# A two-layer hybrid mixer: its first stage put into a written order, with rounded first folds and condition vectors in PSUM

## The chip, the core and the metric

The kernel runs on one core of a Trainium2 chip. The core has a matrix engine (TensorE, called PE in the profile; its weight loads are listed apart as PEld), three elementwise engines (VectorE = DVE, ScalarE = ACT, GpSimd = POOL) and SyncE (SP), which issues nearly all DMA transfers. Each engine works through its own list in order and waits on semaphores where it needs another's result. The metric is the device time of one execution in microseconds; lower is better.

## What is computed

Batch 1, 1024 latent tokens (S), 256 context tokens (C), width 1024 (D), two layers. All data is float32. The parts of the reference that matter here:

```python
sc, scc = jax.nn.silu(c), jax.nn.silu(c_ctx)
shift, scale, gate = jnp.split(sc @ mod_w[0] + mod_b[0], 3, axis=-1)
hx = modulate(rmsnorm(x, norm_g[0]), shift[:, None], scale[:, None])
shift_c, scale_c, gate_c = jnp.split(scc @ mod_w[0] + mod_b[0], 3, axis=-1)
hc = modulate(rmsnorm(ctx, norm_g[0]), shift_c, scale_c)

def even_mixer(h, h0, p):                       # layer 0
    va, vg, ga, xb, gb = jnp.split(h @ p["w_in"], [...], axis=-1)
    y_a = conformer_conv(va, vg, p) * jax.nn.silu(ga)   # u = va*sigmoid(vg), 31-tap conv, layernorm, silu
    y_b, hT = rglru_branch(xb, p, h0, True)             # 4-tap conv, two gates in two directions, scan
    y_b = y_b * jax.nn.silu(gb)
    return jnp.concatenate([y_a, y_b], axis=-1) @ p["w_out"], hT
```

The context goes only through the `xb` columns and gives the scan its start. In layer 1 a pooling mixer follows; the product of its input weights with its group weights does not depend on the tokens, and the kernel works it out ahead ("folds"): `wfold[g]` is `wu[g]` times `grp[g]`, for four groups g.

## The kernel before

**Tiles.** Channels lie on the 128 partitions, tokens along the free axis; D is 8 tiles (KT) of 128 channels. A weight tile is 128 x 1024 (512 KB). For precision most products are done three times on rounded operands: a value is split into a high part, rounded to the matmul type fp32r by a copy on ACT, and a low part, the difference, worked out on POOL or DVE; then high x high, high x low and low x high are summed in PSUM (`mm3_steps`, line 128, and `mm3_fixed`, line 522). PSUM has eight banks: four rotate under the name `mm` (`psum`, line 87), two form the wide tile `xb` (`wide`, line 91), two more are `c0` and `c1` (`banks`, line 95).

**First stage, lines 297 to 501.** The two condition vectors are spread over the partitions by a one-row product and end in SBUF as `cL` (latents) and `cC` (context). For 6 of the 8 channel tiles (KD = 6), `modulation(k)` (line 344) loads rows k and 8 + k of the transposed modulation weights and makes four dot products on DVE, two rows by two vectors. For the last two tiles `mod_row` (line 365) makes the same numbers on TensorE from `modW`. `x_load` (line 408) loads a tile of x and adds its squares; `rstd_cols` (line 196) makes the reciprocal root of the mean square of all tokens, spread over the partitions. `modulate(k)` (line 384) then scales a tile of x (DVE), rounds it to `h0h` (ACT) and makes the low part `h0l` (DVE). The context takes the same way (`ctx_load`, `ctx_scale`, `ctx_split`). Meanwhile TensorE folds groups 0 and 1 with `fold_whole` (line 271): 64 matmuls of 512 columns on unrounded float32, each of which the profile records as two. Here a planner orders the instructions of each engine, and only the loads are chained (`load`, line 108).

**Second stage, lines 740 to 890.** From the first `vg` product on, nearly everything passes through `on` (line 506), which ties each instruction behind the one before it on its engine: the order of the text is the order of the engine. Loop j from 0 to 7 makes `vg`, `va` (48 matmuls each), the context part `xbc` of tile j + 1 (24 of 256 columns), and then the twelve gate steps of tile j (`gate_steps`, line 725: three matmuls and one Sigmoid on ACT each), between which stand the 48 matmuls of `xb` for tile j + 1. DVE has the four-tap convolution (`other_taps`, line 674), `u = va * sg`, the scans (`rec_scan`), and in between steps of the 31-tap convolution (`conv`, line 574; 49 steps for a tile j below 5, 50 above), which `fill(n)` (line 651) puts in, n at a time. At j = 0 the eight rows of the gate part of the modulation are loaded and dotted too (line 779), and the loop ends with `fill(19)` (line 836).

**After it** come the products `gb`, the output product `wob` (with `fill(7)` behind each half, line 1209), and at m = 5 the layer norm's mean (`ln_mean`, line 1216), which needs all convolutions done. From there to the end nothing is touched by the change.

Of the kernel before, what the change touches and what calls it, by code (L numbers as in the profile page):

```python
# [9 lines left out]
F32 = mybir.dt.float32  # L10
# [5 lines left out]
P = 128  # L16
S = 1024
# [29 lines left out]
KD = 6  # L47
KR = KT - KD
KW = 4 // ((KR + 1) // 2)


# [4 lines left out]
def body(ctx, tc, xT, ctxT, cc, ccol, modT, modW, win, gw, wout, wu, grp, wg, wo1, small, edge, ident, outT):  # L56
# [37 lines left out]

    def banks(name, n):
        if n % 2:
            t = wide(name)
            return [t[:, h] for h in HALF]
        return [pc.tile([P, H], F32, tag=f"c{i}", name=f"{name}_{i}") for i in range(2)]
# [69 lines left out]
    def decay_rates():  # L169
        nc.scalar.activation(sa, lam, AF.Abs)  # L170
        nc.scalar.activation(sa, sa, AF.Exp, scale=-1.0)
        nc.vector.tensor_scalar(out=sb, in0=sa, scalar1=2.0, scalar2=None, op0=add)
        nc.vector.reciprocal(sb, sb)
        nc.vector.tensor_tensor(out=sz, in0=sa, in1=sb, op=mult)
        nc.vector.tensor_tensor(out=sb, in0=sz, in1=sz, op=mult)
        nc.vector.memset(sa, 1.0 / 17.0)
        for n in range(7, -1, -1):
            nc.vector.tensor_tensor(out=sa, in0=sa, in1=sb, op=mult)
            nc.vector.tensor_scalar(out=sa, in0=sa, scalar1=1.0 / (2 * n + 1), scalar2=None, op0=add)
        nc.vector.tensor_tensor(out=sa, in0=sa, in1=sz, op=mult)  # L180
        nc.vector.tensor_scalar(out=sb, in0=lam, scalar1=-1.0, scalar2=0.0, op0=mult, op1=ALU.max)
        nc.vector.scalar_tensor_tensor(out=sa, in0=sa, scalar=2.0, in1=sb, op0=mult, op1=add)
        nc.vector.tensor_scalar(out=chalf, in0=sa, scalar1=4.0, scalar2=None, op0=mult)
        nc.vector.tensor_scalar(out=cneg, in0=sa, scalar1=-8.0, scalar2=None, op0=mult)
# [86 lines left out]
    def fold_whole(g, out_tile, g_tile, w_tile):  # L271
        gs = []
        for i in range(2):
            raw = g_tile(f"graw_{g}_{i}")
            load(raw, grp[g, i])
            gs += [raw[:, 0:H], raw[:, H:D]]
        yield
        for kp in range(KT // 2):
            w = w_tile(f"wu_{g}_{kp}")
            load(w, wu[g, kp])  # L280
            for s in range(2):
                ps = psum(f"fold_{g}_{kp}_{s}")
                for i in range(4):
                    kc = slice(i * 2 * P + s * P, i * 2 * P + (s + 1) * P)
                    nc.tensor.matmul(ps, w[:, kc], gs[i], start=(i == 0), stop=(i == 3))  # L285
                dst = wfold[g][:, :, 2 * kp : 2 * kp + 2, :]
                o = out_tile(f"fo_{g}_{kp}_{s}")
                nc.scalar.copy(o, ps)
                nc.sync.dma_start(dst[:, :, s, :].rearrange("m p c -> p m c"),
                                  o.rearrange("p (m c) -> p m c", c=P))  # L290
            yield


    EVAC = 1000


    cpool = tc.alloc_tile_pool(name="cpool", bufs=1)
    cth = [cpool.tile([P, D], F32R, name=f"cth{i}") for i in range(2)]
    ctl = [cpool.tile([P, D], F32R, name=f"ctl{i}") for i in range(2)]
    cL = cpool.tile([P, D], F32, name="cL")  # L300
    hh, hl, ch, cl = [], [], [], []
    with ExitStack() as sctx:
        fpool = sctx.enter_context(tc.tile_pool(name="fpool", bufs=6))
        gpool = sctx.enter_context(tc.tile_pool(name="gpool", bufs=4))
        spool = sctx.enter_context(tc.tile_pool(name="spool", bufs=1))

        def fo_tile(name):
            return fpool.tile([P, H], F32, tag="fo", name=name)

        def g_tile(name):  # L310
            return gpool.tile([P, D], F32, tag="g", name=name)

        raws = [0]

        def raw_tile(name):
            tag = ("wr", "wh", "wl")[raws[0] % 3]
            raws[0] += 1
            return wpool.tile([P, D], F32, tag=tag, name=name)

        folds = (u for g in range(2) for u in fold_whole(g, fo_tile, g_tile, raw_tile))  # L320

        def fold_some(n):
            for _ in range(n):
                next(folds, None)

        cC = spool.tile([P, D], F32, name="cC")
        cx = [spool.tile([P, D], F32, name=f"cx_{i}") for i in range(2)]


        xs = []  # L330
        acc = [atile("ssq0"), atile("ssq1")]
        accc = spool.tile([P, C], F32, name="ssqc")

        def sumsq(acc_, v, n, first, name, eng):
            if first:
                nc.scalar.activation(acc_[:, :n], v, AF.Square)
            else:
                q = ttile(name)
                nc.scalar.activation(q[:, :n], v, AF.Square)
                eng.tensor_tensor(out=acc_[:, :n], in0=acc_[:, :n], in1=q[:, :n], op=add)  # L340

        junk = spool.tile([P, D], F32, name="junk")

        def modulation(k, between=lambda: None):
            raws_ = []
            for m in (k, KT + k):
                raws_.append(dtile(f"mod0_{m}"))
                load(raws_[-1], modT[0, m])
                if m == k:
                    between()  # L350
            for m, raw in zip((k, KT + k), raws_):
                for i, vec in enumerate((cL, cC)):
                    nc.vector.scalar_tensor_tensor(out=junk, in0=raw, scalar=1.0, in1=vec, op0=mult, op1=mult,
                                                   accum_out=m0[:, i, m : m + 1])
            nc.vector.scalar_tensor_tensor(out=a0[:, :, k], in0=m0[:, :, KT + k], scalar=mb1[:, k : k + 1],
                                           in1=col(O_NG + k).to_broadcast([P, 2]), op0=add, op1=mult)
            v = m0[:, :, k]
            nc.vector.tensor_tensor(out=v, in0=v, in1=col(O_MB + k).to_broadcast([P, 2]), op=add)

        idx = spool.tile([P, P], F32, name="idx")
        ccv = spool.tile([P, KT, 2], F32, name="ccv")

        def mod_row(j):
            ps = psum(f"modr_{j}")[:2, : KR * P]
            for q in range(KT // KW):
                raw = dtile(f"modw_{j}_{q}")
                load(raw[:, : KW * KR * P], modW[j, q])
                for e in range(KW):  # L370
                    k = KW * q + e
                    nc.tensor.matmul(ps, ccv[:, k], raw[:, e * KR * P : (e + 1) * KR * P],
                                     start=(k == 0), stop=(k == KT - 1))
            row = ttile(f"modrow_{j}")[:2, : KR * P]
            nc.scalar.copy(row, ps)
            pst = psum(f"modt_{j}")[:, : 2 * KR].rearrange("p (m c) -> p c m", c=2)
            for e in range(KR):
                nc.tensor.matmul(pst[:, :, e], row[:, e * P : (e + 1) * P], idx[:2, :2], start=True, stop=True)
            ms = slice(j * KT + KD, (j + 1) * KT)
            nc.vector.scalar_tensor_tensor(out=m0[:, :, ms], in0=pst, scalar=1.0 / D,  # L380
                                           in1=col(O_MB + ms.start, KR).unsqueeze(1).to_broadcast([P, 2, KR]),
                                           op0=mult, op1=add)

        def modulate(k):
            t = xs[k]
            shift = m0[:, 0, k : k + 1]
            for h in range(2):
                nc.vector.scalar_tensor_tensor(out=t[:, HALF[h]], in0=t[:, HALF[h]], scalar=a0[:, 0, k : k + 1],
                                               in1=rx[h], op0=mult, op1=mult)
            th, tl = dtile(f"h0h_{k}", F32R), dtile(f"h0l_{k}", F32R)  # L390
            nc.scalar.activation(th, t, AF.Identity, bias=shift)
            nc.vector.scalar_tensor_tensor(out=tl, in0=t, scalar=shift, in1=th.bitcast(F32), op0=add, op1=sub)
            hh.append(th)
            hl.append(tl)

        last_cast = [None]

        def modulate_ctx(k):
            i, q4 = k // 4, k % 4
            cs = slice(q4 * C, (q4 + 1) * C)  # L400
            nc.gpsimd.tensor_scalar(out=cx[i][:, cs], in0=cx[i][:, cs], scalar1=a0[:, 1, k : k + 1],
# [1571 lines left out]
```

## Time and profile before

| | us |
|---|---|
| median of 3 runs | 1290.15 (1288.58 to 1293.81) |
| span of the profiled execution | 1287.8 |
| TensorE busy | 1271.1 |
| VectorE busy | 1141.3 |
| ScalarE busy | 640.6 |
| GpSimd busy | 354.3 |

The span runs from the first to the last instruction of one execution; the run's time holds a little more around it. A row of the views that group instructions reads: line, engine, operation, output from inputs, shape, count, then busy time, the mean of one in ns, and the engine's idle time just before them with what ended it. Many rows have line 510, since `on` records everything there; the tile names tell them apart (`wh_va` is the high part of weight tile `va`, `wl_va` its low part, `wr_va` the raw load). Matmuls overlap in their pipeline: one of 512 columns is shown with 390 ns, while 48 in a row take 10.88 us.

### The profile page before, as it was taken

What the parts mean: (1) busy time and instruction counts of PE and PEld (TensorE: products, weight loads), DVE (VectorE), ACT (ScalarE), POOL (GpSimd) and SP (SyncE); (2) the same over time, 40 slices, a digit from 0 to 9 for tenths busy, and PEclk for the clock granted to TensorE, in tenths of its full rate; (3) what the DMA queues carried; (4) which work ended last, traced back from release to release, by engine and by line L of the source; (5) the groups of instructions that cost most, each with busy time, mean ns of one, the idle gap of its engine ahead of it and who ended that gap; (6) DMA issues with size and microseconds to landing.
All of it is one profiled execution on the core that took longest, in us unless ns stands there. A gap on an engine that the chain in (4) does not pass through costs nothing.

```text
span 1287.8 us, 15841 instructions
## 1 busy us (share of the span) xinstructions
PE 1271.1 (99%) x5650; PEld 1027.5 (80%) x5650; DVE 1141.3 (89%) x1775; ACT 640.6 (50%) x941; POOL 354.3 (28%) x180
## 2 busy tenths in 40 slices
PE   8999999999999999999999999999999999999997
PEld 4468888888888888888887888888888888878886
DVE  7979999999999999988789667999999997887876
ACT  5343656666657623227426345834444444654543
POOL 3063655675558603443220023000000000000002
PEclk9999999999999999999999999999999999999999
DMA  9934111121212133543555356243333324777723
GB/s 371 358 114 157 58 41 63 44 74 42 66 41 90 50 115 107 168 147 113 172 174 192 127 185 203 87 155 127 110 132 131 123 96 157 245 247 258 296 83 131
DMA packets 83075, 181.87 MB, mean 141 GB/s; under 512 B 7858, under 2 KB 27826, under 8 KB 82996
## 3 DMA queue, kind: packets, MB, share of 16 engines
q1 hardware_dynamic: 74548, 176.67, 40.1%
q10 hardware_dynamic: 8448, 4.20, 1.1%
q8 instruction: 44, 0.72, 0.2%
q14 instruction: 35, 0.29, 0.1%
HBM read 136.79 MB, written 44.04 MB: 140 GB/s over the span
## 4 chain that ended last, share of the span: by engine, by line
PE 86%; DVE 6%; DMA 5%; ACT 1%; issue 1%; SPq 0%; POOL 0%; POOLq 0%; DVEq 0%; ACTq 0%
PE vg L510 7%; PE wob L510 7%; PE gb L510 7%; PE va L510 7%; PE xb L510 6%; PE g L510 4%; PE fold L285 3%; PE ga L510 2%; PE qb_v L1000 2%; PE qb_v L1001 2%; PE qb_v L998 2%; PE xbc L510 2%; PE qb_g L1000 2%; PE qb_g L1001 2%; PE qb_g L998 2%; DMA x<-xT 1%
## 5 line engine op out<-in xcount | busy, mean ns | idle before, releaser
L510 DVE SCALAR_TENSOR_TENSOR conv<-u,sm,conv 128x505 f32<-128x505 f32 (+6 forms) x224 | 153.9, 748 | 0.9
L1762 POOL TENSOR_TENSOR o<-x,rr 128x256 f32<-128x256 f32 (+1 forms) x10 | 9.4, 971 | 445.7 <-ACT rr L1698 443.8
L510 POOL TENSOR_TENSOR l<-l,l 128x1280 f32<-128x1280 f32 (+1 forms) x23 | 64.0, 2798 | 91.8 <-DVE l L510 65.5
L510 ACT ACTIVATE l<-g,sm 128x512 f32<-128x512 f32 (+1 forms) x96 | 58.7, 619 | 57.7 <-PE g L510 57.0
L285 PE MATMUL fold<-graw,wu 128*128 128x512 f32 x128 | 58.0, 614 | 2.3 <-DMA wu<-wu 2.3
L102 ACT CAST wq_g<-wr_g 128x512 fp32r<-128x512 f32 x48 | 28.3, 622 | 48.4 <-DVE wr_g L979 17.6
L285 PEld LDWEIGHTS fold<-graw,wu 128*128 128x128 f32 x128 | 25.1, 198 | 33.7 <-issue 32.7
L510 PE MATMUL vg<-h0h,wl_vg 128*128 128x512 f32 x128 | 50.0, 390 | 0.0
L510 PE MATMUL wob<-ybh,wh_wob 128*128 128x512 f32 x128 | 49.9, 390 | 0.0
L510 PE MATMUL vg<-h0h,wh_vg 128*128 128x512 f32 x128 | 49.8, 389 | 0.0
L510 PE MATMUL gb<-h0l,wh_gb 128*128 128x512 f32 x128 | 49.8, 389 | 0.0
L510 PE MATMUL gb<-h0h,wh_gb 128*128 128x512 f32 x128 | 49.8, 389 | 0.0
L510 PE MATMUL wob<-ybh,wl_wob 128*128 128x512 f32 x128 | 49.8, 389 | 0.0
L510 PE MATMUL vg<-h0l,wh_vg 128*128 128x512 f32 x128 | 49.8, 389 | 0.0
L510 PE MATMUL wob<-ybl,wh_wob 128*128 128x512 f32 x128 | 49.8, 389 | 0.0
L510 PE MATMUL va<-h0h,wh_va 128*128 128x512 f32 x128 | 49.8, 389 | 0.0
L510 PE MATMUL va<-h0l,wh_va 128*128 128x512 f32 x128 | 49.8, 389 | 0.0
L510 PE MATMUL va<-h0h,wl_va 128*128 128x512 f32 x128 | 49.8, 389 | 0.0
L510 PE MATMUL gb<-h0h,wl_gb 128*128 128x512 f32 x128 | 49.8, 389 | 0.0
L510 DVE TENSOR_TENSOR_SCAN l<-l,l 128x256 f32<-128x256 f32 (+1 forms) x32 | 48.7, 1521 | 1.1
L103 POOL TENSOR_TENSOR wl_wu<-wr_wu,wh_wu 128x1024 fp32r<-128x1024 f32 x8 | 19.2, 2417 | 106.9 <-ACT wh_wu L102 104.4
L510 POOL TENSOR_TENSOR l<-l,uc 128x1280 f32<-128x1280 f32 x16 | 48.1, 3032 | 0.0
(642 smaller groups left out, 4344.0 us busy)
## 6 DMA issues: line engine op xcount, KB each, us to landing
mod<-modT SPq DMA_DIRECT2D x20, 512.0 KB, 5.5
x_part<-xp SPq DMA_DIRECT2D x32, 256.0 KB, 3.1
mod<-modT SPq DMA_DIRECT2D x32, 256.0 KB, 3.1
wr_v<-wfold SPq DMA_DIRECT2D x16, 512.0 KB, 4.0
wr_g<-wg SPq DMA_DIRECT2D x16, 512.0 KB, 4.2
wr_wo<-wo SPq DMA_DIRECT2D x16, 512.0 KB, 4.6
y_b<-y SPq DMA_DIRECT2D x24, 256.0 KB, 3.4
y_t<-y SPq DMA_DIRECT2D x24, 256.0 KB, 2.9
```

What stands on the lines that cost most here:

```text
L102: return (nc.scalar.copy(hi, src), eng.tensor_tensor(out=lo, in0=src, in1=hi.bitcast(F32), op=sub))
L103: eng.tensor_tensor(out=lo, in0=src, in1=hi.bitcast(F32), op=sub))
L285: nc.tensor.matmul(ps, w[:, kc], gs[i], start=(i == 0), stop=(i == 3))
L510: last[eng] = f(*args, **kw)
L998: nc.tensor.matmul(ps, hi, xh[k], start=(first and k == 0), stop=False, skip_group_check=not first)
L1000: nc.tensor.matmul(ps, hi, xl[k], start=False, stop=False, skip_group_check=not first)
L1001: mm = nc.tensor.matmul(ps, lo, xh[k], start=False, stop=(k == KH - 1), skip_group_check=not first)
L1762: nc.gpsimd.tensor_tensor(out=outs[k // per][:, k % per], in0=x1[k][:, cols], in1=rr, op=mult)
```

## The change

The first stage is written anew, and every instruction of it now passes through `on`, so that TensorE, DVE, ACT and POOL each follow the order of the text from the first instruction on, and SP that of `load`.

- The folds of groups 0 and 1 are done with split operands, 24 matmuls of fp32r for each of the 8 weight tiles, in place of 8 of float32. The four raw group tiles are split by ACT and DVE, the eight weight tiles by ACT and POOL. The stores stand in the chain of loads.
- The condition vectors stay in PSUM: `cvec[0]` in the wide tile `xb`, `cvec[1]` in a second wide tile `cw`. `cL` is a copy of the first, used for the gate rows and later.
- `mod_row` and its inputs are gone; all 8 tiles have dot products on DVE, for tiles 5 to 7 the latents' first and the context's later.
- The products `xb0` and `vg0` of the latents run together, channel tile by channel tile.
- Behind them stand `va0`, the context's normalisation, `u0`, the decay rates, the gate rows, the gate steps of tile 0 for the latents with `xb1` between them, then `xbc0`, `xbc1` and the gate steps for the context. Iteration j = 0 of the loop is gone, and where it ended with `fill(19)` (and had `fill(3)` before) stands `fill(4)`.

```diff
+    def wide2(name):
+        return pc.tile([P, S], F32, tag="cw", name=name)
...
+    cvec = [wide("c_0"), wide2("c_1")]
...
+    def fold_part(n, s, part):
+        g = n // 4
+        w = fw[n][part == 2]
+        for i in range(4):
+            kc = slice(i * 2 * P + s * P, i * 2 * P + (s + 1) * P)
+            hi, lo = gpair[g][i // 2]
+            x = lo if part == 1 else hi
+            pe(fps_[n][s], w[:, kc], x[:, HALF[i % 2]], start=(part == 0 and i == 0), stop=(part == 2 and i == 3))
...
+    def mod_dots(m, vecs=(0, 1)):
+        for i in vecs:
+            vec(nc.vector.scalar_tensor_tensor, out=mraw[m] if i else junk, in0=mraw[m], scalar=1.0, in1=cvec[i],
+                op0=mult, op1=mult, accum_out=m0[:, i, m : m + 1])
...
+    load_w("vg0", win[KT])
+    load_mod(5)
...
+    mod_dots(5, (0,))
+    for h in range(2):
+        r, t = roots[h], ttile(f"dg_x{h}")
+        vec(nc.vector.reciprocal, out=r, in_=r)
+        vec(nc.vector.tensor_tensor, out=t.rearrange("p (c t) -> p c t", t=P),
+            in0=idx.unsqueeze(1).to_broadcast([P, H // P, P]), in1=r.unsqueeze(2).to_broadcast([P, H // P, P]), op=mult)
...
+    rest = [lambda: (mod_dots(KT + 5, (0,)), mod_ready(0, 4, 6)), lambda: mod_dots(6, (0,)), lambda: mod_dots(KT + 6, (0,)),
+            lambda: (mod_ready(0, 6, 7), mod_dots(7, (0,))), lambda: (mod_dots(KT + 7, (0,)), mod_ready(0, 7, KT)),
+            lambda: (mod_dots(5, (1,)), mod_dots(KT + 5, (1,))), lambda: None, lambda: None]
+    scale_x(0)
+    high_x(0)
+    for k in range(KT):
+        if k < KT - 1:
+            scale_x(k + 1)
+            high_x(k + 1)
+        low_x(k)
+        rest[k]()
+        if k == 0:
+            xb = wide("xb0")
+            vg = [psum(f"vg0_{h}") for h in range(2)]
+        kc = slice(k * P, (k + 1) * P)
+        for part in range(3):
+            for (hi, lo), ps in ((w, [xb[:, h] for h in HALF]), (wg0, vg)):
+                for h in range(2):
+                    pe(ps[h], (lo if part == 1 else hi)[:, kc], (hl if part == 2 else hh)[k][:, HALF[h]],
+                       start=(k == 0 and part == 0), stop=(k == KT - 1 and part == 2))
...
+    first_tap(0, xb, uc[:, C:])
+    sg = [ttile(f"sg0_{h}") for h in range(2)]
+    for h in range(2):
+        act(sg[h], vg[h], AF.Sigmoid)
+    other_taps(0, xb, uc[:, C:])
+    wva = split_w("va0", (cth[0], ctl[0]))
+    uh, ul = utile("uh0", F32R), utile("ul0", F32R)
+    cast(uh[:, C:], uc[:, C:])
+    wnext = split_w("xb1")
+    gp(out=ul[:, C:], in0=uc[:, C:], in1=uh[:, C:].bitcast(F32), op=sub)
+    va = [psum(f"va0_{h}") for h in range(2)]
+    all_of(mm3_fixed(va[0], wva, (hh, hl), HALF[0]))
+    msc = psum("ms_c")[:, :C]
+    pe(msc, ones, accc, start=True, stop=True)
+    all_of(mm3_fixed(va[1], wva, (hh, hl), HALF[1]))
...
+    load(rawg, gw[0])
...
+    load(raw, win[KT + 1])
+    lrows = {m: lrow(m) for m in range(2 * KT, 3 * KT)}
...
+    act(sq, msc, AF.Sqrt, bias=eps_r)
+    lrow_dots(2 * KT)
+    u = xtile("u0")
...
+    vec(nc.vector.tensor_tensor, out=u[:, HALF[0]], in0=va[0], in1=sg[0], op=mult)
+    vec(nc.vector.reciprocal, out=accc, in_=sq)
+    for i in range(2):
+        v = cx[i].rearrange("p (k n) -> p k n", n=C)
+        vec(nc.vector.tensor_tensor, out=v, in0=v, in1=accc.unsqueeze(1).to_broadcast([P, 4, C]), op=mult)
+        for q4 in range(4):
+            k, cs = 4 * i + q4, slice(q4 * C, (q4 + 1) * C)
+            on("pool", nc.gpsimd.tensor_scalar, out=cx[i][:, cs], in0=cx[i][:, cs], scalar1=a0[:, 1, k : k + 1],
+               scalar2=m0[:, 1, k : k + 1], op0=mult, op1=add)
...
+        cast(cth[i], cx[i])
+        gp(out=ctl[i], in0=cx[i], in1=cth[i].bitcast(F32), op=sub)
+    vec(nc.vector.tensor_tensor, out=u[:, HALF[1]], in0=va[1], in1=sg[1], op=mult)
...
+    decay_rates()
...
+    for m in range(2 * KT + 1, 2 * KT + 4):
+        lrow_dots(m)
...
+    for n, _ in enumerate(gate_steps(0, (gwh, gwl), (uh, ul), gates, ((C, H), (C + H, H)))):
+        while done < 16 * (n + 1) // 8:
+            next(steps)
+            done += 1
...
+    all_of(mm3_fixed(xc, w, (ch, cl), slice(0, C)))
...
+    all_of(mm3_fixed(xcn, wnext, (ch, cl), slice(0, C)))
+    first_tap(0, xc, uc[:, :C])
+    other_taps(0, xc, uc[:, :C])
+    cast(uh[:, :C], uc[:, :C])
+    gp(out=ul[:, :C], in0=uc[:, :C], in1=uh[:, :C].bitcast(F32), op=sub)
...
+    first_tap(1, xcn, ucn[:, :C])
+    other_taps(1, xcn, ucn[:, :C])
+    for m in range(2 * KT + 4, 3 * KT):
+        lrow_dots(m)
...
+    all_of(gate_steps(0, (gwh, gwl), (uh, ul), gates, ((0, C),)))
...
+    rec_input(state, 0)
+    w = raw_split(raw, "vg1")
+    at_rest()
+    fill(4)
```

912 lines of the change are left out of this document (488 added, 424 removed).

## The prediction

> **What bounds the kernel now.** I read the page first, then the busy time by stretches, the chain of work that ended last, and DVE's instructions in order of time.
>
> ```profile
> span 1287.8 us, 15841 instructions
> PE 1271.1 (99%) x5650; PEld 1027.5 (80%) x5650; DVE 1141.3 (89%) x1775; ACT 640.6 (50%) x941; POOL 354.3 (28%) x180
> ...
> PE 86%; DVE 6%; DMA 5%; ACT 1%; issue 1%; SPq 0%; POOL 0%; POOLq 0%; DVEq 0%; ACTq 0%
> ```
>
> TensorE looks like the only bound. The stretches (from:to, length, then busy PE, PEld, DVE, ACT, POOL with counts, clock, DMA share, GB/s) correct that:
>
> ```profile
> 0.00:55.00 55.00, 49.50 (x143) 23.86 (x144) 44.84 (x78) 25.10 (x43) 10.52 (x11) 1.00 0.99 376
> ...
> 80.70:102.40 21.70, 21.70 (x107) 18.21 (x106) 13.89 (x33) 9.75 (x12) 14.72 (x12) 1.00 0.46 172
> 102.40:137.50 35.10, 35.10 (x173) 29.74 (x172) 34.85 (x50) 12.12 (x18) 11.74 (x5) 1.00 0.22 75
> 137.50:180.00 42.50, 42.50 (x206) 35.86 (x205) 42.01 (x56) 26.50 (x30) 25.02 (x10) 1.00 0.16 54
> ...
> 521.00:566.00 45.00, 45.00 (x201) 37.24 (x200) 44.37 (x72) 11.59 (x15) 24.32 (x15) 1.00 0.47 158
> ```
>
> Until 55 us the DMA share is 0.99: loads pace the stage. From 102 us on DVE is as full as TensorE (42.01 of 42.5), also in the output product (44.37 of 45). A delay of DVE is therefore not hidden by a faster TensorE. The chain (start, us, what) dates TensorE's side:
>
> ```profile
> 46.27 27.66 PE fold L285 x64
> ...
> 74.37 6.87 PE fold L285 x16
> ...
> 105.96 10.88 PE va L510 x48
> 116.84 2.87 PE xbc L510 x24
> ...
> 137.56 10.88 PE vg L510 x48
> ...
> 166.66 0.35 PE g L510 x3
> ...
> 508.55 65.28 PE wob L510 x288
> ```
>
> Folds fill TensorE until 81 us, then products run without a gap, 0.227 us for a matmul of 512 columns, and tile 1 begins at 137.56. DVE's side (start, us):
>
> ```profile
> 124.58 14.76 DVE L510 SCALAR_TENSOR_TENSOR conv<-u,sm,conv 128x504 f32<-128x504 f32 x22
> 139.24 1.28 DVE L510 SCALAR_TENSOR_TENSOR uc<-xb,sm,uc 128x1022 f32<-128x1022 f32 x1
> ...
> 165.04 1.50 DVE L510 SCALAR_TENSOR_TENSOR uc<-xbc,sm,uc 128x254 f32<-128x254 f32 x3
> ...
> 568.60 0.41 DVE L510 CAST mu0h<-lnsum 128x512 fp32r<-128x512 f32 x1
> ...
> 574.10 0.69 DVE L510 TENSOR_TENSOR mu1l<-lnsum,mu1h 128x512 fp32r<-128x512 f32 x1 [2.68 <-PE mu L510]
> ```
>
> Two couplings are to be seen. DVE frees the bank of `xbc` at 166.5 and the fourth gate step takes it at 166.66: DVE has 0.2 us in hand at tile 1. And DVE begins the layer norm's mean at 568.6, while TensorE ends its first 288 `wob` matmuls at 573.8: with 1.2 us for both parts of the mean's operand DVE has 4.0 us in hand there.
>
> **The change: until the first products.** The rows of the first stage (grouped; mean in ns last before the bar):
>
> ```profile
> L285 PE MATMUL fold<-graw,wu 128*128 128x512 f32 x11 | 7.4, 840 | 2.3 <-DMA wu<-wu 2.3
> ...
> L353 DVE SCALAR_TENSOR_TENSOR junk<-mod,cL 128x1024 f32<-128x1024 f32 x12 | 15.2, 1266 | 1.7 <-DMA mod<-modT 0.8 <-ACT cL L433 0.8
> L388 DVE SCALAR_TENSOR_TENSOR x<-x,a,ms_x 128x512 f32<-128x512 f32 x16 | 10.8, 744 | 0.5 <-PE ms_x L211 0.5
> L392 DVE SCALAR_TENSOR_TENSOR h0l<-x,m,h0h 128x1024 fp32r<-128x1024 f32 x8 | 10.5, 1335 | 0.0
> ...
> L372 PE MATMUL modr<-modw,ccv 128*2 128x256 f32 x32 | 7.2, 379 | 0.0
> ```
>
> TensorE's own work falls: the folds from 64 float32 matmuls at 2 x 0.433 us (27.66 / 64 a record), 55.4 us, to 192 at 0.227, 43.5 us; and 7.2 us of `modr` go. Neither is on the path, for products wait for other things. The order of loads puts 33 half-megabyte loads, 7 stores of 0.26 MB and 0.3 MB of small ones, 19.4 MB, before and with modulation row 5; at 376 GB/s that is 51.6 us. DVE has the dot product of that row in front of the two diagonals: 1.3, then 1.5 for reciprocals and diagonals and 1.0 for spreading them (estimates from the half-width DVE op at 0.68, which is 10.8 / 16, and two float32 matmuls): x is scaled from 55.4 on.
>
> The products are written tile by tile, but `xb0` is the next tile in the banks of `cvec[0]`, and four of that vector's dot products (rows 6, 14, 7, 15) stand in `rest[1]` to `rest[4]`, behind it. TensorE's first matmul, and in its order all others, must wait for the last. Until then DVE runs 12 half scalings (8.1), 5 low parts at 1.31 (6.6), 5 dots at 1.27 (6.3) and two sets of small adds (0.8): 21.8, so products begin at 77. No row has a dot with a PSUM operand: the half-width scaling with one (0.68) doubles to 1.35, the SBUF dot is 1.27 and I take that; a single bank read without gain or loss. Ends: 1.15 and 1.35 a dot, 1 us here either way. The 96 matmuls take 21.8. By then TensorE has stood since its folds ended near 58 (the eighth fold's last 8 matmuls stand behind the spreading). The first 11 fold records after a thin start took 7.4 us, 0.67 each against 0.433, so that start cost 2.6; I take 2.0 here, 1.0 before `va0` and 1.5 at the gates (0 to 2.6 each). Call the end of `xb0` and `vg0` T: 77 + 21.8 + 2.0 = 101. Before, these 96 matmuls would end at 80.7 + 21.8 = 102.5. The gain up to here is 1.5 us.
>
> The Trainium skill (TensorE: Matmul & The Clock Gate, Part 1: The HAM clock gate) says that the array runs at half clock for some 3.4 us after an idle window of that length. The clock column reads 1.00 in the very stretch with the slow records, so the slow start agrees and the column does not show it; an estimate by that page is 1.7 us for each of four restarts, 6.8 in place of my 4.5.
>
> **From T to tile 1.** These rows price it, the engines' groups first and then the loads, with us from issue to landing last:
>
> ```profile
> L510 ACT ACTIVATE uc<-xb,sm 128x1024 f32<-128x1024 f32 x2 | 2.4, 1206 | 0.7 <-PE xb L510 0.7
> L510 ACT ACT_TABLE_LOAD x1 | 1.3, 1283 | 0.0
> L510 ACT ACTIVATE sg<-vg 128x512 f32<-128x512 f32 x2 | 1.2, 600 | 0.8 <-PE vg L510 0.8
> L510 ACT CAST wh_va<-wr_va 128x1024 fp32r<-128x1024 f32 x1 | 1.0, 1044 | 0.0
> L510 POOL TENSOR_TENSOR wl_va<-wr_va,wh_va 128x1024 fp32r<-128x1024 f32 x1 | 2.4, 2395 | 5.8 <-ACT wh_va L510 5.8
> L510 DVE SCALAR_TENSOR_TENSOR uc<-xb,sm,uc 128x1023 f32<-128x1023 f32 x2 | 2.6, 1283 | 0.1
> L193 DVE RECIPROCAL ssqc<-sq_c 128x256 f32<-128x256 f32 x1 | 1.7, 1746 | 0.0
> L443 DVE TENSOR_TENSOR cx<-cx,ssqc 128x1024 f32<-128x1024 f32 x2 | 2.4, 1222 | 0.0
> L401 POOL TENSOR_SCALAR cx<-cx,a,m 128x256 f32<-128x256 f32 x8 | 5.2, 670 | 7.6 <-DVE cx L443 7.6
> L172 DVE TENSOR_SCALAR sb<-sa 128x16 f32<-128x16 f32 x1 | 4.4, 4351 | 7.0 <-ACT sa L171 7.0
> L510 POOL TENSOR_TENSOR l<-l,uc 128x1280 f32<-128x1280 f32 x1 | 3.0, 2974 | 0.0
> L510 DVE SCALAR_TENSOR_TENSOR l<-l,cL 128x1024 f32<-128x1024 f32 x8 | 15.3, 1970 | 0.0
> ```
>
> ```profile
> l<-modT SPq DMA_DIRECT2D x6, 512.0 KB, 6.5
> ...
> wr_vg<-win SPq DMA_DIRECT2D x1, 512.0 KB, 3.4
> wr_va<-win SPq DMA_DIRECT2D x1, 512.0 KB, 4.3
> ```
>
> Wait one, before `va0`: on ACT its cast stands behind the first tap, a table load and two Sigmoids (1.2 + 1.3 + 1.1 + 1.0, with handovers T + 4.8), and POOL's low part ends at T + 7.3. `va0` and the context's sum end at T + 19.5.
>
> Wait two, at the gates: DVE's taps (3 x 1.28) end at T + 5.3, ACT rounds `uh` and `xb1` by T + 7.4, POOL's low part of `xb1` at T + 9.9 frees the raw buffer that SP needs for `vg1`; the gate row 16 is queued behind that load and lands 4.3 later, at T + 14.8 (3.4 for a lone load in the same list, 6.5 in a bunch: -1 to +2). Behind its dot on DVE stand `u0`, the reciprocal and the context's scaling: first half at T + 19.6. POOL's four scalings (2.6), ACT's cast (1.1), POOL's low part (2.4), four more scalings and the second cast give T + 29.6; then come Abs, Exp and two table loads, and only then the first gate's Sigmoid, at T + 33.3. TensorE fills its four banks with gate steps and half of `xb1` by T + 27.7 (36 matmuls, 8.2) and waits 5.6. The other half ends at T + 43.1, `xbc0` and `xbc1` at T + 48.9.
>
> Wait three, before `vg1`: tap, taps, cast and low part of the context (0.6 + 1.5 + 0.4 + 0.7) pass beside `xbc1`; POOL's `rec_input` (3.0, from T + 51) stands ahead of the low part of `vg1` (2.4): T + 56.5. TensorE is at tile 1 as if from 157.3, 19.7 later than 137.56.
>
> DVE: Exp arrives at T + 31.3, the first small op sits out POOL's low part as the 4.35 us row did (T + 32), 22 small ones at 0.2 (T + 37), three gate rows (T + 40.7), the wait for `xbc0` and its taps (T + 48.3), the next taps (T + 51.2), four gate rows beside `rec_input` (1.3 each, 1.97 at worst: T + 56.5), one sum (T + 57.4), and seven convolution steps at 0.67 (14.76 / 22): the taps of tile 1 start at T + 62.1 = 163.1 where they started at 139.24. That is 23.9 later, less the 0.2 in hand: 23.7. It is the larger, so TensorE loses 4 us more in tile 1.
>
> **Behind it.** `fill(4)` for 3 + 19 steps moves 18 steps, 12.0 us, to the `wob` stage. In tiles 1 to 7 nothing changes; at the mean DVE had 4.0 us in hand, so TensorE stands 8.0 longer there.
>
> **Sum:** 23.7 + 8.0 = 31.7 on the span of 1287.8, 1319.5. The median stands 2.35 above that span, so **1322 us**.
>
> **The rivals.** (a) The bank holds nothing up: T = 55.4 + DVE's whole list of 31 us (16 half scalings, 8 low parts, 7 dots) + 1.5 = 88, all else as above: 1309. For: the text order; against: four dots on the old tile. Chance 0.12. (b) Faster: TensorE is the bound throughout, T = 88 and the three waits vanish because ACT and POOL run ahead; then 102.5 - 88 = 14 us are won, 1276. For: 86% of the chain; against: each wait is a queue written out. 0.08. (c) No change: T = 88, DVE's lag is taken up by spare time I do not see, and only TensorE's own waits count, 88 + 56.3 - 137.56 = 7, less 4 if the gate row is there in time: 1293. 0.08. (d) Worse: all restarts cost 2.6, gate rows 1.97 each, rows land late: 1335 and up. 0.10. That leaves 0.62 for my forecast, decided at the point where the taps of tile 1 start: before 131 us the change would win (8 us being lost again at the mean), after that it loses.
>
> Range: 1303 (all of (a)) to 1337; (b), (c) and half of (d) lie outside. Within 0.5%, 6.5 us, is about what a measurement of this kernel cannot tell from no change: faster 0.08, same 0.08, slower 0.84.
>
> **What would show it.** Right: a gap in TensorE between the last fold near 58 us and the first `xb0` matmul near 77, released by DVE's dot; idle TensorE before `va0` (7 us), inside the gate steps of tile 0, and at `vg1`; taps of tile 1 near 163; idle TensorE before `mu`. Wrong: `xb0` starting near 57, gate Sigmoids ahead of the context's casts, or DVE idle in tiles 1 to 7.

## The result and the profile after

| | before | after |
|---|---|---|
| median of the runs beside each other, us | 1289.37 (4 runs, 1287.05 to 1293.81) | 1370.33 (4 runs, 1368.69 to 1374.21) |
| ratio after / before, 95% interval | | 1.0627 [1.0595, 1.066] |
| span of the profiled execution, us | 1287.8 | 1366.9 |

The change costs 81 us; 32 were predicted, and the time lies far above the range (1303 to 1337). First the page of the changed kernel: its span, the busy time, the chain by engine, and the group of convolution taps (busy us, mean ns of one, then idle us before them).

```profile
span 1366.9 us, 15894 instructions
PE 1278.4 (94%) x5674; PEld 1047.1 (77%) x5674; DVE 1175.1 (86%) x1789; ACT 651.4 (48%) x947; POOL 370.2 (27%) x187
...
PE 58%; DVE 23%; issue 7%; ACT 4%; POOL 4%; DMA 4%; POOLq 0%; SPq 0%; DVEq 0%; ACTq 0%
...
L276 DVE SCALAR_TENSOR_TENSOR conv<-u,sm,conv 128x505 f32<-128x505 f32 (+6 forms) x224 | 168.0, 750 | 6.6
```

TensorE was 99% busy and had 86% of the chain; it has 58% now, and DVE 23% where it had 6%. The stretches (from:to, length, then busy PE, PEld, DVE, ACT, POOL with counts, clock, DMA share, GB/s) show where TensorE stands:

```profile
64.00:87.25 23.25, 2.84 (x11) 1.71 (x11) 21.31 (x34) 8.21 (x8) 2.35 (x1) 0.67 0.69 236
87.25:111.00 23.75, 23.75 (x95) 19.44 (x96) 8.87 (x14) 4.38 (x6) 4.67 (x4) 0.90 0.00 1
111.00:130.00 19.00, 13.33 (x47) 9.98 (x46) 14.17 (x18) 8.88 (x10) 8.39 (x4) 0.82 0.48 179
130.00:146.00 16.00, 9.77 (x44) 7.75 (x42) 5.92 (x9) 5.24 (x7) 9.97 (x10) 0.92 0.33 133
...
185.00:227.50 42.50, 35.18 (x163) 28.34 (x163) 41.19 (x55) 24.66 (x29) 18.91 (x8) 0.97 0.13 42
```

Before 87.25 us it is nearly idle (2.84 of 23.25), it has gaps up to 146 us, and in tile 1, which begins at 185 us on DVE's side, it is busy for 35.18 of 42.5 where the kernel before had 42.50: 7.3 us, where the prediction had 4 of waiting in tile 1 and none from there to the mean. TensorE's first matmuls behind each gap (start, us, group, idle time in front and what ended it):

```profile
87.25 1.19 PE L276 MATMUL xb<-h0h,wh_xb 128*128 128x512 f32 x2 [20.41 <-DVE junk L276]
115.80 0.58 PE L276 MATMUL va<-h0h,cth 128*128 128x512 f32 x1 [4.22 <-ACT cth L276]
...
146.49 0.80 PE L276 MATMUL g<-uh,wh_gw 128*128 128x512 f32 x1 [6.72 <-ACT l L276]
...
166.27 0.50 PE L276 MATMUL vg<-h0h,wh_vg 128*128 128x512 f32 x1 [1.50 <-ACT wh_vg L276]
...
171.84 0.79 PE L276 MATMUL vg<-h0h,wl_vg 128*128 128x512 f32 x1 [4.83 <-POOL wl_vg L276]
```

These are the four waits of the prediction, each with the releaser it named: the bank (DVE's last dot product), the cast of `va0` (and 1.45 us more for its low part), the gate Sigmoids behind the context, and the low part of `vg1` behind POOL's product. DVE at the two points that the prediction dated, and then TensorE where it leaves the layer norm, in the kernel before and after:

```profile
184.96 1.28 DVE L276 SCALAR_TENSOR_TENSOR uc<-xb,sm,uc 128x1022 f32<-128x1022 f32 x1
...
649.63 0.42 DVE L276 CAST mu0h<-lnsum 128x512 fp32r<-128x512 f32 x1
```

```profile
599.34 5.61 PE ga L510 x24
```

```profile
678.56 5.61 PE ga L276 x24
```

The taps of tile 1 start 45.7 us later (139.24 before; 23.9 predicted), the mean 81.0 later (568.60; 36 would have followed), and TensorE reaches `ga` 79.2 later. So all of the loss (79.1 us on the span) is made before 680 us, and a good part of it between tile 1 and the mean, where the prediction had nothing but the 18 moved steps.

The convolution steps themselves say where. One step takes as long as before (750 and 748 ns), but 15 in a row take longer:

```profile
189.84 11.79 DVE L276 SCALAR_TENSOR_TENSOR conv<-u,sm,conv 128x507 f32<-128x507 f32 x15
```

```profile
187.51 10.45 DVE L510 SCALAR_TENSOR_TENSOR conv<-u,sm,conv 128x510 f32<-128x510 f32 x15
```

The first is the changed kernel, the second the kernel before: (11.79 - 0.75) / 14 = 0.79 us from start to start against 0.69, and 0.667 in the longest run of the kernel before, the 22 steps in 14.76 us. Before, most steps begin before the one in front of them has ended (0.667 is less than 0.75); after, each begins only behind that end.

### The profile page after: what moved, and what is told of

The parts are those of the page before. It is cut to its first block, busy times and chain, and to the rows that moved or that the text cites. A ratio compares the mean times of both kernels' runs of the same rounds, so it can differ in the third digit from the quotient of the medians.

```text
span 1366.9 us, 15894 instructions
## 1 busy us (share of the span) xinstructions
PE 1278.4 (94%) x5674; PEld 1047.1 (77%) x5674; DVE 1175.1 (86%) x1789; ACT 651.4 (48%) x947; POOL 370.2 (27%) x187
## 4 chain that ended last, share of the span: by engine, by line
PE 58%; DVE 23%; issue 7%; ACT 4%; POOL 4%; DMA 4%; POOLq 0%; SPq 0%; DVEq 0%; ACTq 0%
DVE conv L276 9%; PE vg L276 4%; DVE l L276 3%; PE va L276 2%; PE xb L276 2%; DVE u L276 2%; PE g L276 2%; PE ga L276 2%; PE ga L131 2%; PE ga L129 2%; PE qb_v L1170 2%; PE qb_v L1167 2%; PE qb_v L1169 2%; PE gb L276 2%; PE ga L130 2%
## 5 line engine op out<-in xcount | busy, mean ns | idle before, releaser
L276 DVE SCALAR_TENSOR_TENSOR conv<-u,sm,conv 128x505 f32<-128x505 f32 (+6 forms) x224 | 168.0, 750 | 6.6
L276 PE MATMUL xb<-h0h,wh_xb 128*128 128x512 f32 x128 | 49.8, 400 | 20.4 <-DVE junk L276 20.4
L276 DVE SCALAR_TENSOR_TENSOR conv<-cL,wsum,conv 128x506 f32<-128x506 f32 (+3 forms) x70 | 52.4, 749 | 2.0
L276 PE MATMUL xb<-h0l,wh_xb 128*128 128x512 f32 x128 | 49.6, 398 | 0.0
L276 PE MATMUL xb<-h0h,wl_xb 128*128 128x512 f32 x128 | 49.3, 395 | 0.0
L98 ACT CAST wq_v<-wr_v 128x512 fp32r<-128x512 f32 x48 | 28.3, 621 | 36.3 <-DMA wr_v<-wfold 14.5
```

Of the source, the lines that this page charges most:

```text
L98: return (nc.scalar.copy(hi, src), eng.tensor_tensor(out=lo, in0=src, in1=hi.bitcast(F32), op=sub))
L276: last[eng] = f(*args, **kw)
```

## The experiments

**The theory after the result.** The new tile `cw` also changed the helper `banks`, and with it the whole convolution, which the list of the change does not say. `banks` used to give a convolution's two accumulators, `acc_` and `late`, as two PSUM tiles, and now gives the halves of one. The taps go to them in turns. If dependencies are kept by tile, each step now waits for the one in front of it, whose result it does not use, and consecutive steps no longer overlap. Rivals: the steps are slow because the late start has put the engines out of step; or the cost is there but TensorE hides it. The rest, about 58 us, would be the first stage: the bank, SP's queue, POOL beside the gate rows, the chain of the context, the moved steps.

**One part alone: the joined tile in the kernel before.**

```diff
+    def wide2(name):
+        return pc.tile([P, S], F32, tag="cw", name=name)
     def banks(name, n):
-        if n % 2:
-            t = wide(name)
-            return [t[:, h] for h in HALF]
-        return [pc.tile([P, H], F32, tag=f"c{i}", name=f"{name}_{i}") for i in range(2)]
+        t = wide(name) if n % 2 else wide2(name)
+        return [t[:, h] for h in HALF]
```

> The kernel before with one edit of the change alone: the two accumulators of a convolution tile (and the other pairs that the same helper gives out) are halves of one double-bank PSUM tile in place of two tiles. Theory: a step then waits for the step in front of it, which it does not depend on; steps start 0.785 us apart instead of 0.66. About 43 of the 51 steps of each of 8 tiles have such a neighbour: 344 x 0.12 = 41 us on DVE, less the 4 us in hand, so about +37 (range +28 to +45), 1317 to 1334 us, conv rows of 128x505 to 128x508 in runs at 0.78 spacing, TensorE with gaps in tiles 1 to 7. Rival one: the joined tile costs nothing and the slow steps of the changed kernel come from its late start (engines out of step): 1289 within 0.5%, spacing 0.66. Rival two: it costs, but TensorE hides it: spacing 0.78 and at most +5.

Measured: 1320.04 us beside 1290.18, ratio 1.023 [1.0215, 1.0245]: +30. The same 22 steps as in the prediction's first row of DVE:

```profile
124.44 17.29 DVE L511 SCALAR_TENSOR_TENSOR conv<-u,sm,conv 128x504 f32<-128x504 f32 x22
```

17.29 us for 14.76: (17.29 - 0.75) / 21 = 0.788 from start to start, at an unchanged 750 ns each, and the first stage ends where it did (taps of tile 0 at 99.55, before 99.96). Both rivals fall. The size lies at the low end. Counted in the two traces, 273 steps directly follow another step. In the kernel before 232 of them, 29 a tile and not 43, start before the one in front has ended, 0.653 us behind its start on average; with the joined tile none does, and the average is 0.786. So DVE's steps take 232 x 0.133 = 31 us more, the mean starts 32.2 us later (600.77), and TensorE reaches `ga` 30.4 later.

**The joined tile undone in the changed kernel.** The double bank stays for the second condition vector and is given up before the first convolution.

```diff
+    pv = tc.alloc_tile_pool(name="pv", bufs=1, space=PSUM)
+    pcv = []
...
     def wide2(name):
-        return pc.tile([P, S], F32, tag="cw", name=name)
+        return pv.tile([P, S], F32, tag="cw", name=name)
...
+    pv.release()
+    pcv.append(ctx.enter_context(tc.tile_pool(name="pcv", bufs=1, space=PSUM)))
     state, uc = (0, uc, gates, roots), ucn
```

> The changed kernel with the pairs as two tiles again, from the first convolution step on (the double-bank tile stays for the second condition vector and is given up before). First theory (dependency between neighbours): spacing back to 0.66, 33 to 45 us less, 1325 to 1337 us, and what is left over the kernel before (36 to 48 us) is the first stage, taps of tile 1 still at 185. Rival (late start is the cause): 1370 within 0.5%. A third reading: the loss of the first stage alone, 45.7 us at the taps of tile 1 plus 12 of moved steps less 4 in hand, would leave 1343.

Measured: 1348.43 us, ratio 1.0452 [1.0434, 1.0469]: 21.9 less than the changed kernel. (The kernel before stood at 1290.18 beside it and at 1289.37 beside the changed kernel, so such differences carry about 1 us more.)

```profile
186.09 1.27 DVE L281 SCALAR_TENSOR_TENSOR uc<-xb,sm,uc 128x1022 f32<-128x1022 f32 x1
...
190.97 10.18 DVE L281 SCALAR_TENSOR_TENSOR conv<-u,sm,conv 128x507 f32<-128x507 f32 x15
...
628.85 0.42 DVE L281 CAST mu0h<-lnsum 128x512 fp32r<-128x512 f32 x1
```

The same 15 steps fall from 11.79 to 10.18 us; tile 1 starts where it did, and the mean comes 20.8 us sooner. The direction of the first theory holds, its 33 to 45 does not: the third reading's 1343 is nearest. So of 81 us the joined tile is 22, and 59 are the first stage with its 18 moved steps.

DVE's steps shorten by 31 us here too, but not all of it arrives. From the taps of tile 1 to those of tile 7 it takes 269.3 us in the changed kernel, 252.4 here and 254.8 in the kernel before. Without the joined tile TensorE has no gap left in these tiles and sets the pace again (tiles 2 to 6, changed kernel first; the first two numbers behind the stretch are its length and TensorE's busy time):

```profile
229.00:454.00 225.00, 218.70 (x1030) 181.38 (x1030) 218.21 (x276) 132.10 (x150) 136.38 (x57) 0.99 0.16 53
```

```profile
229.00:438.00 209.00, 209.00 (x1007) 176.49 (x1006) 204.18 (x274) 128.41 (x147) 133.29 (x56) 1.00 0.17 55
```

**Half the neighbours dependent, two tiles.** To tell the dependency from the tile, the kernel before got its taps two by two:

```diff
-        for n in range(NT + 1):
-            if n < NT - 1 and n != 7:
-                tap(acc_, ue, w(2 * n + 1), n - 7)
-                yield
-            if n != 8:
-                tap(late, uo, w(2 * n), n - 8)
-                yield
+        one = [(acc_, ue, w(2 * n + 1), n - 7) for n in range(NT - 1) if n != 7]
+        two = [(late, uo, w(2 * n), n - 8) for n in range(NT + 1) if n != 8]
+        while one or two:
+            for q in (one, two):
+                for args in q[:2]:
+                    tap(*args)
+                    yield
+                del q[:2]
...
-            tap((acc_, late)[i % 2], ub, both(n), n - 7)
+            tap((acc_, late)[i // 2 % 2], ub, both(n), n - 7)
```

> The kernel before, its two accumulator tiles kept, with one edit: the taps of a convolution tile go two by two (two on the first accumulator, two on the second) instead of in turns, so that every other step follows one whose result it needs. Dependency theory: the dependent half start 0.785 us apart and the others 0.66, about half of what the joined tile cost alone: joined was +30 and 4 us of DVE's reserve, so 34/2 - 4 = 13, 1300 to 1306. Rival (the joined tile costs by itself, not by the dependency between neighbours): 1290 within 0.5%, spacing 0.66 throughout.

Measured: 1297.88 us beside 1290.13, ratio 1.0071 [1.0052, 1.009].

```profile
124.54 15.81 DVE L510 SCALAR_TENSOR_TENSOR conv<-u,sm,conv 128x506 f32<-128x506 f32 x22
```

(15.81 - 0.75) / 21 = 0.717, between 0.667 and 0.788, without any joined tile. The single steps are plainer than the mean. These are the first pair, which shares nothing, and the next, in which the second step needs the first one's result:

```profile
124.54 1.39 DVE L510 SCALAR_TENSOR_TENSOR conv<-u,sm,conv 128x506 f32<-128x506 f32 x2
```

```profile
125.19 1.52 DVE L510 SCALAR_TENSOR_TENSOR conv<-u,sm,conv 128x504 f32<-128x504 f32 x2
```

All 21 starts of this run go on so, 0.65 to 0.66 us and 0.77 to 0.79 by turns. The kernel before shows the same twice: of the 21 starts in its row of 14.76 us, 19 are 0.65 to 0.66 us apart and two 0.79, the two at which both neighbours use one accumulator. The dependency is what costs, and the joined tile costs by making every neighbour one. The total moved by 8 us, not by 13: 105 of the 232 free steps lost their early start, 13.9 us on DVE; of that 11.5 arrive at the mean (580.07) and 7.7 at TensorE's `ga`, which fits the 4 us that DVE had in hand there.

**The bank alone.** The last five dot products of the first condition vector read its copy in SBUF:

```diff
-            vec(nc.vector.scalar_tensor_tensor, out=mraw[m] if i else junk, in0=mraw[m], scalar=1.0, in1=cvec[i],
+            vec(nc.vector.scalar_tensor_tensor, out=mraw[m] if i else junk, in0=mraw[m], scalar=1.0, in1=cvec[i] if src is None else src,
...
-    rest = [lambda: (mod_dots(KT + 5, (0,)), mod_ready(0, 4, 6)), lambda: mod_dots(6, (0,)), lambda: mod_dots(KT + 6, (0,)),
+    rest = [lambda: (mod_dots(KT + 5, (0,), cL), mod_ready(0, 4, 6)), lambda: mod_dots(6, (0,), cL), lambda: mod_dots(KT + 6, (0,), cL),
...
```

> The changed kernel with the last five dot products of the first condition vector reading its copy in SBUF, so that its bank pair is free for the first products before them. Bank theory: the first xb0 matmul starts near 69 instead of 87.25, behind the first low part; products then follow DVE's list (3.9 us for each of 8 tiles) and end near 97 instead of 111; taps of tile 1 near 171 instead of 185, total 10 to 15 us less: 1355 to 1360. Rival: the products end 14 us sooner but wait for weights, gate row and context that do not move: less than 4 us gained. Second rival: the bank is not what the first matmul waits for: nothing changes.

Measured: 1360.3 us, ratio 1.0537 [1.0519, 1.0554]: 10.0 less. TensorE's first product and DVE's taps of tile 1:

```profile
69.28 0.83 PE L276 MATMUL xb<-h0h,wh_xb 128*128 128x512 f32 x2 [1.79 <-ACT h0h L276]
```

and on DVE:

```profile
175.24 1.28 DVE L276 SCALAR_TENSOR_TENSOR uc<-xb,sm,uc 128x1022 f32<-128x1022 f32 x1
```

The first product starts at 69.28 instead of 87.25. The products then follow DVE's list and end at 101.0 instead of 111.4, not at the 97 expected, and 9.7 us arrive at tile 1. The bank is shown, at 10 us.

**SP's order alone.** In the changed kernel SP stands from 47 to 55.5 us at the load of `vg0`, whose buffer POOL has not yet emptied, and row 5 waits behind it (start, us, of each issue; then DVE's dot product of that row and the first scalings):

```profile
46.75 0.43 SPq L108 DMA_DIRECT2D wfold<-fo  x1
55.49 0.33 SPq L108 DMA_DIRECT2D wr_vg<-win  x1
55.86 0.43 SPq L108 DMA_DIRECT2D mod<-modT  x1
```

```profile
60.83 1.22 DVE L276 SCALAR_TENSOR_TENSOR junk<-mod,c 128x1024 f32<-128x1024 f32 x1 [6.41 <-DMA mod<-modT]
...
64.16 2.95 DVE L276 SCALAR_TENSOR_TENSOR x<-x,a,ms_x 128x512 f32<-128x512 f32 x4 [0.40 <-PE ms_x L276]
```

```diff
-    load_w("vg0", win[KT])
     load_mod(5)
...
     load_mod(KT + 7)
+    load_w("vg0", win[KT])
```

> The changed kernel with the load of the first vg weight put behind the six last modulation rows, so that SP no longer stands 8 us before them. If row 5 is what holds x: it lands near 52 as predicted (60.8 seen), x is scaled from 56 to 57, and the whole gains 6 to 8 us. If TensorE's order holds x too (the spreading of the roots stands behind 16 matmuls of the eighth fold, which begin only at 55.4 behind the sums of squares): the row lands near 52, x is scaled from 62 to 63.5, and the gain is 1 us or less in the total.

Measured: 1366.9 us (one run). Row 5 is issued at 47.97 and waits for nobody, but x is scaled only 2.0 us sooner (DVE's rows of this run, then TensorE's of the same time):

```profile
55.28 1.22 DVE L276 SCALAR_TENSOR_TENSOR junk<-mod,c 128x1024 f32<-128x1024 f32 x1
...
62.12 2.92 DVE L276 SCALAR_TENSOR_TENSOR x<-x,a,ms_x 128x512 f32<-128x512 f32 x4 [2.02 <-PE ms_x L276]
```

```profile
55.73 3.33 PE L276 MATMUL fold<-cth,wh 128*128 128x512 f32 x8
58.86 1.45 PE L276 MATMUL fold<-ctl,wh 128*128 128x512 f32 x4
60.15 1.07 PE L276 MATMUL fold<-cth,wl 128*128 128x512 f32 x4
61.06 1.88 PE L276 MATMUL ms_x<-dg_x,ones 128*128 128x512 f32 x4
```

Two things held x: the row, and the 16 matmuls of the eighth fold in front of the spreading. With one gone the other holds it. The total is 3 us below the median of the changed kernel, which a single run does not show to be a gain.

**The gate rows away from POOL.** DVE's dot products of rows 21 to 23 and the add behind them, in the changed kernel:

```profile
165.65 3.92 DVE L276 SCALAR_TENSOR_TENSOR l<-l,cL 128x1024 f32<-128x1024 f32 x1
...
169.51 3.36 DVE L276 SCALAR_TENSOR_TENSOR l<-l,cL 128x1024 f32<-128x1024 f32 x1
...
172.79 3.92 DVE L276 SCALAR_TENSOR_TENSOR l<-l,cL 128x1024 f32<-128x1024 f32 x1
...
176.76 2.23 DVE L276 TENSOR_TENSOR m<-m,sm 128x8 f32<-128x8 f32 x1
```

```diff
-    for m in range(2 * KT + 1, 2 * KT + 4):
+    for m in range(2 * KT + 1, 3 * KT):
         lrow_dots(m)
...
-    for m in range(2 * KT + 4, 3 * KT):
-        lrow_dots(m)
...
     all_of(gate_steps(0, (gwh, gwl), (uh, ul), gates, ((0, C),)))
```

> The changed kernel with the dot products of gate rows 20 to 23 moved ahead of the context's taps, next to those of rows 17 to 19, where DVE idles 6.5 us and POOL does nothing. Contention theory: three of these four took 3.92, 3.36 and 3.92 us beside POOL's products, and the small add behind them 2.23; moved they take 1.15 to 1.22 each in idle time, so the taps of tile 1 start 12 to 14 us sooner, at 171 to 173, and the total falls by as much if DVE sets it: 1356 to 1358. Rival: TensorE is late too (vg1 waits for POOL's low part) and hides most of it: taps sooner, but under 6 us gained. Second rival: the rows are slow wherever they stand: taps at 181 or later.

Measured: 1363.48 us, ratio 1.0571 [1.0552, 1.0589].

```profile
159.88 1.22 DVE L276 SCALAR_TENSOR_TENSOR l<-l,cL 128x1024 f32<-128x1024 f32 x1
...
176.05 1.27 DVE L276 SCALAR_TENSOR_TENSOR uc<-xb,sm,uc 128x1022 f32<-128x1022 f32 x1
```

The rows take 1.22 us. In this execution the first stage ended 2.9 us later (taps of tile 0 at 115.36 against 112.45), so the way from there to tile 1 is the fair measure: 60.7 us for 72.5, 11.8 less, about what was expected. At tile 1 itself it is 8.9, and in the median total 6.9 us arrive, short of the 12 to 14 expected. The start lies ahead of the edit and is a difference between executions; the other 2 us are not placed.

**Steps brought back.** 12 of the 18 moved steps run while DVE waits for the Exp.

```diff
     whole_[0] = 1
+    fill(12)
     decay_rates()
```

> The changed kernel with 12 of the 18 convolution steps brought back to tile 0, into the 9.9 us in which DVE waits for the Exp of the decay rates (the sum of the two halves of u0 moves behind the first 29 steps). By my step 4 (moved steps come due at the layer norm's mean) nothing changes at the taps of tile 1, and the mean comes 12 x 0.785 = 9.4 us sooner: 1361. Rival: the mean is set by TensorE's lateness and not by DVE's list: no change, 1370.

Measured: 1365.14 us, ratio 1.0578 [1.0547, 1.0608]; taps of tile 1 at 185.52, the mean at 643.71. Tile 1 stays and the mean comes 5.9 us sooner, as the last step of the prediction said in kind. 9.4 were expected: between the taps of tile 7 and the mean 8.3 are gained, and 2.4 had been lost before it (taps of tile 7 at 456.65 against 454.24).

**All five edits.**

> All five edits in the changed kernel: two accumulator tiles again, the last dots from the SBUF copy, the vg load behind the modulation rows, the gate rows moved up, 12 steps brought back. If each repairs its own loss: 22 + 10 + 3 + 13 + 8 = 56 us less, 1314 (1308 to 1320). If several repair the same wait: 1322 or more. Not below the kernel before in either case, since the context's chain (7 us of TensorE's waits at the gates and 12 at va0 and vg1) is not touched.

Measured: 1316.81 us, ratio 1.0212 [1.0193, 1.0232], 53.5 less than the changed kernel; the five alone gave 47.4 together (3.4 of it from a single run). So none repairs what another does already; why it is 6 more than the sum stays open, but the first stage of one and the same order differed by 2.9 us between two executions above. What TensorE still waits for between the first products and tile 1:

```profile
102.66 0.80 PE L281 MATMUL va<-h0h,cth 128*128 128x512 f32 x1 [4.20 <-ACT cth L281]
105.11 0.80 PE L281 MATMUL va<-h0h,ctl 128*128 128x512 f32 x1 [1.22 <-POOL ctl L281]
133.35 0.80 PE L281 MATMUL g<-uh,wh_gw 128*128 128x512 f32 x1 [6.22 <-ACT l L281]
...
153.60 0.50 PE L281 MATMUL vg<-h0h,wh_vg 128*128 128x512 f32 x1 [1.50 <-ACT wh_vg L281]
157.61 0.80 PE L281 MATMUL vg<-h0h,wl_vg 128*128 128x512 f32 x1 [3.29 <-POOL wl_vg L281]
```

**The three waits too.** To the five edits, with 9 steps brought back for 12, came: the split of `va0`, the context's squares, the gate weights and the gate rows' loads during the first products; the decay rates near 20 us; the context's casts between the gates; the split of `vg1` ahead of POOL's product; and the gate rows' dots against a PSUM copy of the vector.

```diff
+        if k == 1:
+            got["va"] = split_w("va0", (cth[0], ctl[0]))
...
+        if 2 <= k < 6:
+            ctx_square(k - 2)
...
+    c0p = wide2("c0p")
+    cast(c0p, cL)
...
+        if n in (2, 4):
+            i = n // 2 - 1
+            cast(cth[i], cx[i])
...
```

> The five edits, and the waits between the first products and tile 1 taken away as well: the split of va0, the squares and sum of the context, the gate weights and gate rows during the first products; the decay rates in DVE's idle time near 20 us; the context's casts between the gates; the gate rows' dots against a PSUM copy of the vector; the split of vg1 ahead of POOL's product. If the three waits of my prediction (va0, gates, vg1) hold the rest: TensorE runs on from the end of xb0/vg0 (94 to 97) to vg1 in 35 us, taps of tile 1 at 135 to 139, 8 convolution steps fewer than before at that point: 1285 to 1300. If something else holds it (POOL's list, DVE's list): 1305 or more.

Measured: 1301.76 us, ratio 1.0094 [1.0075, 1.0113], 15 us less again. TensorE's waits in the same stretch fall from 16.9 us (the rows above and one of 0.42 at the second gate step) to 1.5 (0.17, 0.42 and 0.93). DVE is what is late: the taps of tile 1 start at 144.72, not at 135 to 139, and before them stand two operations with two SBUF inputs beside POOL's work:

```profile
134.81 1.95 DVE L284 SCALAR_TENSOR_TENSOR edge_junk<-u,sm 128x8 f32<-128x8 f32 x1
...
136.70 3.52 DVE L284 TENSOR_TENSOR cL<-u 128x512 f32<-128x512 f32 x1
```

**Those taken away as well.**

```diff
+    for k in range(2):
+        scale_x(k)
+        high_x(k)
     fold_out(7, 0)
...
     whole_[0] = 1
-    fill(9)
+    at_rest()
+    fill(10)
```

> The kernel of the run before this one (context early) with the waits that its trace still shows taken away: the first two tiles of x are scaled and rounded ahead of the last fold's two evictions (DVE waited 3.3 us for ACT there), the sum of the halves of u0 and its edge stand ahead of the first convolution steps instead of beside POOL's products (1.95 and 3.52 us there), the small add of the gate rows moves behind POOL's last context product (2.00 us there), and tile 0 has 10 steps instead of 9. If these are DVE's own losses, the taps of tile 1 start 9 to 11 us sooner, at 134 to 136 (144.7), TensorE's vg1 at 131 to 133, and the total is 1287 to 1293. If DVE's list is full anyway and TensorE already had its gain: 1297 or more.

Measured: 1297.18 us, ratio 1.005 [1.0035, 1.0066], six runs from 1293.31 to 1299.0. From the taps of tile 0 (103.88) to those of tile 1 (142.93) it now takes 39.1 us, as in the kernel before (39.3). So the way between them is mended, but the total of 1287 to 1293 was missed, since the first stage came later in this execution: folds waited twice for DVE's low part of the second group matrix (3.13 and 3.31 us) where the run before, with the same order there, waited once (1.46). In both runs the decay rates stand in front of that low part, small operations of 0.17 us each. In the run before two of them stood beside POOL's work and took 2.25 and 1.28 us; in this one four did (2.32, 1.27, 1.22 and 2.33), and the low part started at 36.99 instead of 33.72. No version tried is faster than the kernel before.

## Why the prediction was wrong

**The step that failed** is "In tiles 1 to 7 nothing changes". The edit of `banks` was read as a matter of space and not priced at all: 0 where the runs show 22 us of the 81 (30 on its own). It made 232 convolution steps wait for a neighbour whose result they do not use, on the engine that the prediction itself had called full, and tiles 1 to 7 take 269.3 us for 254.8. The row that spoke of it stood in the prediction: 22 steps of 0.75 us in 14.76 us can only be if neighbours overlap.

The other steps, by their own terms (us; T is the end of `xb0` and `vg0` on TensorE, 115.80 - 4.22 = 111.6):

| step | predicted | measured |
|---|---|---|
| x scaled | 55.4 | 64.16 |
| from there to the first product (bank) | 21.6 | 23.1 |
| T | 101 | 111.6 |
| first gate Sigmoid | T + 33.3 | T + 34.2 (145.75) |
| T to the taps of tile 1 | 62.1 | 73.4 |
| taps of tile 1, against before | +23.7 | +45.7 |
| behind them, two tiles | +8.0 | +11.2 |
| joined tile | 0 | +21.9 |
| sum on the span | +31.7 | +78.8 (79.1 seen) |

The "behind them" row is from the run with two tiles: `ga` at 657.34, 58.0 later than before, less 46.85 at its taps of tile 1. It is larger than predicted since the mean comes 13.4 later from tile 1 on, not 12.0, and TensorE made up 2.2 of it and not 4.0.

Right, with their releasers: the bank, the three waits, DVE and not TensorE setting tile 1, the moved steps paid at the mean. The bank costs 10.0 where rival (a) would have had 13. Rivals (a) to (c) fall with that: the bank is in the way, and nothing of TensorE's shorter work is won. Of rival (d) a part came true, the gate rows, and at a higher price than it gave.

Mis-sized are above all two terms. *x scaled*: the estimate divided bytes by a rate, as if SP issued every load at once. SP's queue stood 8 us behind a buffer that POOL had to empty (DMA share 0.42 from 50 to 60 us), and the eighth fold's matmuls stood in front of the spreading; the prediction named the second order without a price, and did not ask which buffers SP's loads depend on. *T to the taps of tile 1*: the four gate rows were taken at 1.3, at worst 1.97, each. That 1.97 was the mean of a group of eight of which five took 1.2 us and three, beside POOL's operations, 3.98, 3.40 and 2.30; in the changed kernel three of these four took 3.92, 3.36 and 3.92. With the rows moved the way is 60.7, from the taps of tile 0, where the prediction had 60.9 (T + 1.2 to T + 62.1).

The restarts of the clock were priced at 4.5 us and cost TensorE 9.3: 2.4 behind the bank, where the prediction had 2.0, then 2.3 before `va0`, 1.9 at the gates and 2.8 at `vg1`. Only the first stands in T; how much of the others reaches tile 1, which DVE sets, is not shown. The column shows them now: behind the first gap matmuls start 0.43 us apart until 92 us, against 0.227 later, and the granted clock (third number from the end) is 0.50:

```profile
87.25:92.00 4.75, 4.75 (x11) 3.77 (x12) 4.72 (x9) 1.15 (x1) 0.00 (x0) 0.50 0.01 3
```

The half clock is as the Trainium skill (TensorE: Matmul & The Clock Gate, Part 1: The HAM clock gate) would have it; the prediction's estimate by that page, 6.8, was nearer than its own 4.5 and still too low.

## What to carry to other kernels

Two accumulators that are written in turns belong in two tiles: halves of one tile make each instruction wait for a neighbour it does not need, and the price (0.13 us on 0.65 here) is paid by an engine's whole list while the duration of one instruction shows nothing; look at start to start. A mean over a group in which some members run beside another engine is no bound for the ones that will: take the disturbed row. And when a wait is taken away, look for the next one in line before counting the gain, in the issuing queue (SP) as much as on the engines.

## What the runs showed of the hardware

Consecutive DVE operations of 0.75 us on 504 to 512 columns start 0.65 to 0.66 us apart when the second needs nothing of the first, and 0.77 to 0.79 when it waits for it. The Trainium skill (VectorE: DVE Perf Modes, The DRAIN you can't avoid) says that a next operation that is not held starts earlier, which agrees; it also reports a test in which a semaphore after each operation cost nothing, and that differs from the 14.76 and 17.29 us for the same 22 steps here, so here the measurement decides.

A dot product with both operands in SBUF took 1.22 us alone and up to 3.92 beside POOL's products, and even an add of 8 columns took 2.23 for 0.15. With one operand in PSUM it did not notice POOL: the eight gate rows against the PSUM copy, between 112.4 and 121.6 us while POOL scaled and split the context from 111.5 on:

```profile
L284 DVE SCALAR_TENSOR_TENSOR l<-l,c0p 128x1024 f32<-128x1024 f32 x8 | 9.2, 1216 | 0.0
```

The Trainium skill (SBUF — State Buffer, SBUF: two separate sides) calls the port pair that the two engines share an exclusive lock, which a DVE operation with two SBUF inputs needs against a POOL operation that reads SBUF, as does one in a two-port mode; the trace agrees, with these numbers.
